# Issuing the retention products of two key tiles and two heads as one run of four, and the group norm's small products further back

## The chip, the cores and the metric

The kernel runs on one core of a Trainium2 chip. The metric is the device time of one execution in microseconds (us): the median of three runs before is 1449.22 us (1446.68 to 1450.26). The profile is of one further execution, whose own time is 1448.63 us and whose span, from the first to the last instruction, is 1446.9 us.

Five engines matter, and each works through its own instructions in program order: TensorE (PE in the profile; PEld is its loading of weights), VectorE (DVE), ScalarE (ACT), GpSimd (POOL), and SyncE (SP), which issues the transfers.

## The reference

A two-layer encoder over 512 tokens of width 1024, in 32-bit floats. Layer 0 mixes tokens with retention and with neighbourhood attention, layer 1 with a state-space (SSD) mixer; each is followed by a feed-forward network (FFN). The two places that matter here, cut down:

```python
# layer 0, retention: per head, every query against every key, weighted by a decay
y = bidir_scan(rq, rk, rv, rv, a_f, a_b)          # = (rq rk^T * decay) rv
mu = mean(y); var = mean((y - mu)**2)             # per head
ret_out = silu(rg) * (y - mu) * rsqrt(var + EPS) * ret_gn_g

# layer 1, SSD: after the scan, per group of 512 channels
y = (y + xh * d_skip) * silu(z)
yg = y * rsqrt(mean(y * y over the group) + EPS) * norm_g
out = yg @ w_out
```

## The kernel before

Activations lie with features on partitions and tokens along the row (128 x 512 tiles). A large product (`mm3`, lines 86 to 88) is three products of split operands, so most of PE's time is in those three lines. Weights come in units of 512 KB (`wunit`): a transfer, a split into a high part on ACT (line 81) and a low part on DVE (line 82).

The kernel is written in a language whose scheduler decides the order of instructions on each engine when the program is built: it takes code order as priority, `high_priority` raises it, and an engine takes what it expects to be ready first. On the chip that order is then fixed, and an engine waits at an instruction whose operands aren't there.

**Layer 0** (`mixer0`) goes through four pairs of heads. The table `PAIRS` gives the order of steps of each pair: five projections (`rq rk nk nq rg`), `d` (the decay tables `toep`, lines 410 to 414), `s0..s3` (scores of one key tile, both heads), `v0..v3` (values of that key tile), `a`, `w` and `o` (the neighbourhood attention), and `n` (the norm over a head's 64 rows). A score step (`ret_scores`) makes two 128 x 512 products a head (lines 423, 424) and masks them on DVE into an `sd` tile (line 426); the `sd` tiles share five buffers with the tiles of the attention and the norm. A value step (`ret_values`, line 434) makes one product for each of the two heads, 64 output rows each: head 0 writes partitions 0 to 63 of the accumulator `y`, head 1 writes 64 to 127. The four value steps of a pair add up in `y`. In the trace each such product has two records on PE, with two weight loads.

**Layer 1** (`mixer1`) goes through four groups of eight heads in the order of `SLOTS`. A step `p` (`pair`, line 757) makes eight small products (line 764) for two heads, again 64 rows for each head, then the gate, the square on ACT (line 770) and the sum of squares `sq` on POOL (line 774). With the last pair of a group, `pair` itself goes on to four one-column products `pss` of the sums (line 782), a DVE step (784) and a POOL power (786) that give the factor `r`. The output projection of a group (`out`, `out_tile`) multiplies by `r` when it leaves PSUM (lines 798, 800, 803). For the last group that projection, `r`, the post norm and the next layer's pre norm follow each other at the end of the mixer.

Of the kernel before, what the change touches and what calls it, by code (L numbers as in the profile page):

```python
# [7 lines left out]
F32 = mybir.dt.float32  # L8
# [3 lines left out]
ALU = mybir.AluOpType  # L12
# [3 lines left out]
P = 128  # L16
S = 512
NT = S // P
D = 1024
KD = D // P  # L20
EPS = 1e-6
# [4 lines left out]
class Env:  # L26
# [57 lines left out]
    def mm3(self, out, lh, ll, rh, rl, first, last):  # L84
        mm = self.nc.tensor.matmul
        mm(out, lh, rh, start=first, stop=False)  # L86
        mm(out, ll, rh, start=False, stop=False)  # L87
        mm(out, lh, rl, start=False, stop=last)  # L88

    def proj_fm(self, out, w, c0=0, c1=S):  # L90

# [161 lines left out]
def log1p_exp_neg(E, alloc, z):  # L253
# [24 lines left out]


PAIRS = (  # L280
# [4 lines left out]
)  # L285


def mixer0(E, w0, w_v, w_fm, tabs, dist_d, logit, gn, bias, w_out, g_post_row, done):
# [3 lines left out]
    nc, tc = E.nc, E.tc  # L292
    with ExitStack() as ctx:
        pool = lambda name, bufs: ctx.enter_context(tc.tile_pool(name=name, bufs=bufs))
        one, two, sd, bp = pool("m0", 1), pool("m0b", 2), pool("m0s", 5), pool("m0n", 2)

        rot = one.tile([P, 2, S], F32, name="rot")
        nc.sync.dma_start(rot, tabs)
# [118 lines left out]
        def ret_scores(p, o, i):  # L417

            o["sd", i] = []
            for h in range(2):  # L420
                ps = E.px.tile([P, S], F32, name="sc", tag="px")
                kt, (qt, ql) = o["rk"][h][:, i * P:(i + 1) * P], o["rq"]
                nc.tensor.matmul(ps, kt, qt[h], start=True, stop=False)
                nc.tensor.matmul(ps, kt, ql[h], start=False, stop=True)
                m = sd.tile([P, S], F32, name="sd", tag="sd")
                nc.vector.tensor_tensor(m, ps, o["toep"][h][:, 384 - i * P:384 - i * P + S], op=ALU.mult)
                o["sd", i].append(m)

        def ret_values(p, o, i):
            if i == 0:  # L430
                o["ry"] = E.px.tile([P, S], F32, name="y", tag="px")
            for h in range(2):
                c = (2 * p + h) * 64
                nc.tensor.matmul(o["ry"][h * 64:h * 64 + 64], rv[:, i, c:c + 64], o["sd", i][h],  # L434
                                 start=i == 0, stop=i == NT - 1)

        def ret_norm(p, o):
            y = o["ry"]
# [82 lines left out]


SLOTS = (
# [4 lines left out]
)  # L528

# [5 lines left out]
def mixer1(E, w_dt, w_fm, cw, dtc, cols, mask, w_out, g_post_row, done):  # L535
# [7 lines left out]
    with ExitStack() as ctx:  # L543
# [168 lines left out]
        def head(o, j):  # L712

            g = o["g"]
            h = g * HPG + j
            pb = [three.tile([P, S], F32, name="pb", bufs=3) for _ in range(2)]
            for dr in range(2):
                nc.sync.dma_start(pb[dr], pd[dr * H + h].partition_broadcast(P))
            e = three.tile([P, NT, C], F32, name="e")
            ds = ys.tile([P, NT, C], F32, name="ds")  # L720
            for c in range(NT):
                cc = slice(c * C, (c + 1) * C)
                nc.scalar.activation(e[:, c], pb[0][:, cc], AF.Identity, scale=-1.0, bias=tok[:, 0, c, h:h + 1])  # L723
                nc.vector.scalar_tensor_tensor(e[:, c], pb[1][:, cc], tok[:, 0, c, H + h:H + h + 1], e[:, c],
                                               op0=ALU.subtract, op1=ALU.max)
                nc.scalar.activation(ds[:, c], um, AF.Identity, scale=ddt[:, c, h:h + 1], bias=tok[:, 1, c, H + h:H + h + 1])  # L726
            nc.scalar.activation(e, e, AF.Exp, scale=-1.0)
            nc.vector.tensor_tensor(e, e, o["gt"], op=ALU.mult)
            nc.vector.tensor_tensor(e, e, ds, op=ALU.mult)  # L729
            o["m"][j] = e  # L730

        def inter(o, q):

# [23 lines left out]
        def pair(o, q):  # L757

            f = o["g"] * 4 + q
            y = o["yi"][q]  # L760
            py = E.px.tile([P, S], F32, name="py", tag="px")
            for c in range(NT):
                for j in range(2):
                    nc.tensor.matmul(py[j * 64:j * 64 + 64, c * C:(c + 1) * C],
                                     o["x"][:, c, (2 * q + j) * 64:(2 * q + j + 1) * 64], o["m"][2 * q + j][:, c],
                                     start=True, stop=True)
            nc.vector.tensor_tensor(y, py, y, op=ALU.add)
            nc.vector.tensor_tensor(y, y, o["t"][6 + q], op=ALU.mult)
            sq = (last if q == 0 else E.tmp).tile([P, S], F32, name="sq", tag="ssq" if q == 0 else "tmp")
# [6 lines left out]
            nc.scalar.activation(yh, y, AF.Identity, scale=col[:, 1, f:f + 1])  # L776
            nc.vector.scalar_tensor_tensor(yl, y, col[:, 1, f:f + 1], yh.bitcast(F32), op0=ALU.mult, op1=ALU.subtract)
            o["y"].append((yh, yl))
            if q == 3:
                pss = E.px.tile([P, NT], F32, name="pss", tag="px")  # L780
                for c in range(NT):
                    nc.tensor.matmul(pss[:, c:c + 1], o["sq"][:, c * C:(c + 1) * C], mean, start=True, stop=True)
                ss = few.tile([P, NT], F32, name="ss", bufs=2)
                nc.vector.tensor_scalar(ss, pss, EPS, None, op0=ALU.add)
                o["r"] = few.tile([P, NT], F32, name="rg", bufs=2)
                nc.gpsimd.tensor_tensor(o["r"], ss, E.mhalf.broadcast_to([P, NT]), op=ALU.pow)

        def out_tile(o, n, t, ws, fin=None):
            g = o["g"]
            ns = slice(n * 512, n * 512 + 512)  # L790
            ps = E.mm.tile([P, 512], F32, name="mm")
            tt = slice(t * P, (t + 1) * P)
            for k in range(4):
                yh, yl = o["y"][k]
                E.mm3(ps, yh[:, tt], yl[:, tt], *ws[k], k == 0, k == 3)
            acc, r = E.x[:, t, ns], o["r"][:, t:t + 1]
            if g == 0:
                nc.scalar.activation(acc, ps, AF.Identity, scale=r)
# [31 lines left out]
        for g, o in enumerate(gs):  # L830
            nx = gs[g + 1] if g + 1 < NG else None
            for step in SLOTS[g].split():
# [8 lines left out]
                elif a == "h":  # L841
                    head(o, i)
                elif a == "i":
                    inter(o, i)
                elif a == "p":
                    pair(o, i)
                elif a == "t":
                    project(o, i)
                elif a == "n":
                    project(nx, i)  # L850
                else:
                    silus(o if a == "S" else nx)
# [3 lines left out]
        def fin(t, n, m):  # L856
# [3 lines left out]
        xt = two.tile([P, 4, 512], R32, name="wo", tag="xt")  # L860
        ws = [E.wunit(w_out[NG - 1, 0, 0]) + E.wunit(w_out[NG - 1, 0, 1]),
              E.wunit(w_out[NG - 1, 1, 0], t4(one, ("state00", "state10", "state01", "state11"))) + E.wunit(w_out[NG - 1, 1, 1], [xt[:, i] for i in range(4)])]
        for t in range(NT):
            for n in range(2):
                out_tile(gs[-1], n, t, ws[n], fin)
            E.finish(TAIL[t], st, done)
        E.late.append(lambda: E.finish(LATE, st, done))

# [143 lines left out]
```

## Time and profile before

| | |
|---|---|
| median of three runs | 1449.22 us |
| the profiled execution | 1448.63 us |
| its span | 1446.9 us |
| layer 0's mixer, from the first scores to its last output product | 88 to 274 us |
| first FFN | 274 to 640 us |
| layer 1's mixer | 665 to 1072 us |
| second FFN, to the end | 1072 to 1447 us |
| records of line 434 / 764 / 782 on PE | 64 / 256 / 32 |

The profile's page gives the busy time of each engine over the span, then groups of instructions by line with the time that the engine stood idle before them and who released it. A timeline row has the start (us from the span's start), the length, the engine, the line, and `xN` for N records merged; records on PE overlap, since an instruction's record goes on after the next has started.

### The profile page before, as it was taken

To read this page: it belongs to the slowest core of one execution; us is meant where nothing else is said; L and a number is where in the kernel's file an instruction comes from. 1 tells how busy PE (TensorE), PEld (TensorE's weight loads), DVE (VectorE), ACT (ScalarE), POOL (GpSimd) and SP (SyncE) were. 2 spreads that over 40 slices of the span, in tenths; PEclk is the share of its full clock that TensorE was granted. 3 is DMA by queue.
4 is the path that set the end of the run, shared out by engine and by line. 5 is a ranking of instruction groups with operands and counts; after the bars stand their busy time and mean duration, and the time that the engine had idled before them with its cause. 6 is when DMAs were issued, how large, how long until landed. Compare 5 with 4: busy or idle time off the path is not lost.

```text
span 1446.9 us, 18038 instructions
## 1 busy us (share of the span) xinstructions
PE 1411.8 (98%) x6848; PEld 1145.2 (79%) x6848; DVE 952.4 (66%) x1484; ACT 724.5 (50%) x1190; POOL 63.0 (4%) x67
## 2 busy tenths in 40 slices
PE   7999999999999999999999999999889999999998
PEld 6877776798888888878688787777778888888886
DVE  7378787766656652347889796899886565564233
ACT  4356665454444441234787775667645444443221
POOL 0010110000000000000000000000020000000000
PEclk9999999999999999999999999999999999999999
DMA  7443221243333323233456354255532333323232
GB/s 253 154 134 88 84 81 44 93 129 91 99 102 90 100 88 109 85 127 114 132 181 180 120 160 145 89 153 156 164 109 84 102 88 102 101 88 102 87 102 88
DMA packets 56951, 166.35 MB, mean 115 GB/s; under 512 B 7200, under 2 KB 7968, under 8 KB 56864
## 3 DMA queue, kind: packets, MB, share of 16 engines
q1 hardware_dynamic: 56864, 165.20, 37.4%
q8 instruction: 54, 0.88, 0.3%
q14 instruction: 33, 0.27, 0.1%
HBM read 157.57 MB, written 5.51 MB: 113 GB/s over the span
## 4 chain that ended last, share of the span: by engine, by line
PE 79%; DVE 9%; ACT 5%; DMA 4%; issue 2%; POOL 1%; SPq 0%; DVEq 0%; POOLq 0%; ACTq 0%
PE mm L86 24%; PE mm L88 24%; PE mm L87 24%; DMA pb<-pd 2%; PE y L434 2%; DVE wlo L82 1%; PE st L701 1%; DVE xf L665 1%; PE pi L745 1%; DMA wst<-in_c_fm 1%; ACT ds L726 1%; PE pt L133 1%; POOL sq L774 1%; ACT whi L81 1%; DVE x L168 1%
## 5 line engine op out<-in xcount | busy, mean ns | idle before, releaser
L86 PE MATMUL mm<-xh,whi 128*128 128x512 f32 (+2 forms) x1216 | 464.3, 382 | 2.3 <-ACT xh L81 1.0
L87 PE MATMUL mm<-xh,wlo 128*128 128x512 f32 (+2 forms) x1216 | 463.6, 381 | 0.7 <-DVE wlo L82 0.7
L88 PE MATMUL mm<-xl,whi 128*128 128x512 f32 (+2 forms) x1216 | 463.5, 382 | 0.0
L82 DVE TENSOR_TENSOR wlo<-wst,whi 128x1024 fp32r<-128x1024 f32 (+1 forms) x214 | 263.5, 1232 | 218.4 <-ACT whi L81 216.0
L81 ACT CAST whi<-wst 128x1024 fp32r<-128x1024 f32 (+1 forms) x214 | 223.6, 1045 | 213.2 <-PE mm L87 156.1
L86 PEld LDWEIGHTS mm<-xh,whi 128*128 128x128 f32 (+1 forms) x1216 | 228.8, 188 | 48.7 <-issue 4.1
L87 PEld LDWEIGHTS mm<-xh,wlo 128*128 128x128 f32 (+1 forms) x1216 | 228.9, 188 | 45.4 <-DVE wlo L82 1.6
L88 PEld LDWEIGHTS mm<-xl,whi 128*128 128x128 f32 (+1 forms) x1216 | 228.2, 188 | 45.9 <-issue 2.9
L218 DVE SCALAR_TENSOR_TENSOR cv<-mm,cwt,cv 128x511 f32<-128x511 f32 x88 | 65.7, 746 | 94.9 <-ACT cv L217 94.9
L86 PE MATMUL mm<-whi,hh 128*128 128x512 f32 x320 | 124.7, 390 | 0.0
L87 PE MATMUL mm<-whi,hl 128*128 128x512 f32 x320 | 124.6, 389 | 0.0
L88 PE MATMUL mm<-wlo,hh 128*128 128x512 f32 x320 | 124.5, 389 | 0.0
L217 ACT ACTIVATE cv<-mm,cwt 128x512 f32<-128x512 f32 x88 | 68.5, 779 | 38.6 <-PE mm L88 38.6
L81 ACT CAST hh<-cv 128x512 fp32r<-128x512 f32 x44 | 27.3, 621 | 100.1 <-DVE cv L226 99.9
L224 ACT ACTIVATE cv<-cv 128x512 f32<-128x512 f32 x44 | 27.8, 632 | 85.8 <-DVE cv L219 85.8
L86 PEld LDWEIGHTS mm<-whi,hh 128*128 128x128 f32 x320 | 60.1, 188 | 12.5
L87 PEld LDWEIGHTS mm<-whi,hl 128*128 128x128 f32 x320 | 60.1, 188 | 12.4
L88 PEld LDWEIGHTS mm<-wlo,hh 128*128 128x128 f32 x320 | 60.1, 188 | 12.3
L219 DVE SCALAR_TENSOR_TENSOR cv<-mm,cwt,cv 128x511 f32<-128x511 f32 x88 | 65.9, 749 | 3.0
L726 ACT ACTIVATE ds<-um,tok,ddt 128x128 f32<-128x128 f32 x128 | 55.7, 484 | 16.6 <-DVE e L729 16.2
L723 ACT ACTIVATE e<-pb,tok 128x128 f32<-128x128 f32 x128 | 42.8, 393 | 15.6 <-DMA pb<-pd 15.1
L82 DVE TENSOR_TENSOR hl<-cv,hh 128x512 fp32r<-128x512 f32 x44 | 30.5, 693 | 28.9 <-ACT hh L81 28.9
(236 smaller groups left out, 1902.3 us busy)
## 6 DMA issues: line engine op xcount, KB each, us to landing
wst<-in_f_up SPq DMA_DIRECT2D x88, 512.0 KB
wst<-in_f_down SPq DMA_DIRECT2D x44, 512.0 KB
wst<-in_c_fm SPq DMA_DIRECT2D x40, 512.0 KB
pb<-pd SPq DMA_DIRECT2D x64, 256.0 KB
wst<-in_ab_fm SPq DMA_DIRECT2D x20, 512.0 KB
gain<-yd SPq DMA_DIRECT2D x32, 256.0 KB
wst<-in_c_out SPq DMA_DIRECT2D x16, 512.0 KB
gain<-in_norms SPq DMA_DIRECT2D x8, 512.0 KB
```

What stands on the lines that cost most here:

```text
L81: self.nc.scalar.copy(hi, src)
L82: self.nc.vector.tensor_tensor(lo, src, hi.bitcast(F32), op=ALU.subtract)
L86: mm(out, lh, rh, start=first, stop=False)
L87: mm(out, ll, rh, start=False, stop=False)
L88: mm(out, lh, rl, start=False, stop=last)
L217: nc.scalar.activation(o, ps, AF.Identity, scale=w(1), bias=w(3))
L218: nc.vector.scalar_tensor_tensor(o[:, 1:], ps[:, :S - 1], w(0), o[:, 1:], op0=ALU.mult, op1=ALU.add)
L219: nc.vector.scalar_tensor_tensor(o[:, :S - 1], ps[:, 1:], w(2), o[:, :S - 1], op0=ALU.mult, op1=ALU.add)
L224: nc.scalar.activation(g, g, AF.Gelu_apprx_tanh)
L434: nc.tensor.matmul(o["ry"][h * 64:h * 64 + 64], rv[:, i, c:c + 64], o["sd", i][h], start=i == 0, stop=i == NT - 1)
L723: nc.scalar.activation(e[:, c], pb[0][:, cc], AF.Identity, scale=-1.0, bias=tok[:, 0, c, h:h + 1])
L726: nc.scalar.activation(ds[:, c], um, AF.Identity, scale=ddt[:, c, h:h + 1], bias=tok[:, 1, c, H + h:H + h + 1])
```

## The change

The value steps `v0` to `v3` become `v0` and `v2`: each makes the four products of two key tiles and two heads, raised in priority by 150. A new helper `together` makes each of the four depend on all four masks (the DVE instructions of line 426), so that none is ready before the others. The steps `v1` and `v3` leave the table, and `v0` now stands behind `a1`. The pool of `sd` tiles has seven buffers in place of five. In layer 1 each of a pair's eight products waits for the decay tiles of both heads. The four `pss` products with what follows leave `pair` and become a step `r` of their own, near the end of each group; in the last group they stand behind the products of the first two output tiles.

```diff
+    def together(self, products, inputs):
+        for m in products:
+            for i in inputs:
+                self.tc.add_manual_dep(m.ins, i.ins.name, mybir.DependencyInfo(
+                    mybir.DependencyClass.Sync, mybir.DependencyReason.DATA))
...
-    "nq rq rk nk rg d s1 s0 a0 v0 a1 v1 w0 s3 s2 a2 v2 a3 w1 w2 v3 n w3 o",
+    "nq rq rk nk rg d s1 s0 a0 a1 v0 w0 s3 s2 a2 a3 v2 w1 w2 n w3 o",
...
-        one, two, sd, bp = pool("m0", 1), pool("m0b", 2), pool("m0s", 5), pool("m0n", 2)
+        one, two, sd, bp = pool("m0", 1), pool("m0b", 2), pool("m0s", 7), pool("m0n", 2)
...
         def ret_values(p, o, i):
+
             if i == 0:
                 o["ry"] = E.px.tile([P, S], F32, name="y", tag="px")
-            for h in range(2):
-                c = (2 * p + h) * 64
-                nc.tensor.matmul(o["ry"][h * 64:h * 64 + 64], rv[:, i, c:c + 64], o["sd", i][h],
-                                 start=i == 0, stop=i == NT - 1)
+            ms, ws = [], []
+            with tc.high_priority(150):
+                for j in (i, i + 1):
+                    for h in range(2):
+                        c = (2 * p + h) * 64
+                        m, w = o["sd", j][h]
+                        ms.append(nc.tensor.matmul(o["ry"][h * 64:h * 64 + 64], rv[:, j, c:c + 64], m,
+                                                   start=j == 0, stop=j == NT - 1))
+                        ws.append(w)
+            E.together(ms, ws)
...
-    "G s0 s1 t6 t7 s2 i0 h0 t8 t9 S h1 p0 i1 n0 h2 h4 h3 p1 i2 n6 n1 h5 n7 i3 n9 p2 N n3 n4 n2 n5 h6 h7 p3 n8 N",
+    "G s0 s1 t6 t7 s2 i0 h0 t8 t9 S h1 p0 i1 n0 h2 h4 h3 p1 i2 n6 n1 h5 n7 i3 n9 p2 N n3 n4 n2 n5 h6 h7 p3 n8 r N",
...
+            ms = [o["m"][2 * q + j] for j in range(2)]
             for c in range(NT):
                 for j in range(2):
-                    nc.tensor.matmul(py[j * 64:j * 64 + 64, c * C:(c + 1) * C],
+                    E.together([nc.tensor.matmul(py[j * 64:j * 64 + 64, c * C:(c + 1) * C],
...
-            if q == 3:
-                pss = E.px.tile([P, NT], F32, name="pss", tag="px")
...
+        def rms(o):
...
+        first = [out_mm(gs[-1], 0, ws[n]) for n in range(2)]
+        rms(gs[-1])
         for t in range(NT):
             for n in range(2):
-                out_tile(gs[-1], n, t, ws[n], fin)
+                out_tile(gs[-1], n, t, ws[n], fin, first[n] if t == 0 else None)
```

On PE, in the second pair of heads (pairs are counted from 0 in what follows, so this is pair 1) at its key tiles 2 and 3, the program before has these rows (`sc` are scores of the neighbourhood attention, `mm` a projection, `pt` transposes, `y<-sd,rv` the value products):

```order
L434 MATMUL y<-sd,rv 64x512
L484 MATMUL pt<-head,e 128x128 x4
L434 MATMUL y<-sd,rv 64x512
L467 MATMUL sc<-nk_1086,nq_1124 128x256
L468 MATMUL sc<-nkl_566,nq_1124 128x256
L467 MATMUL sc<-nk_1086,nq_1124 128x256
L468 MATMUL sc<-nkl_566,nq_1124 128x256
L434 MATMUL y<-sd,rv 64x512
```

And the changed program, at the same place:

```order
L87 MATMUL mm<-xh,wlo 128x512
L88 MATMUL mm<-xl,whi 128x512
L446 MATMUL y<-sd,rv 64x512 x4
L481 MATMUL sc<-nk_1086,nq_1124 128x256
L482 MATMUL sc<-nkl_566,nq_1124 128x256
L481 MATMUL sc<-nk_1086,nq_1124 128x256
L482 MATMUL sc<-nkl_566,nq_1124 128x256
L498 MATMUL pt<-head,e 128x128 x4
```

A fourth lone product stands nine rows above the first piece; the four are one row of four now. In the whole program the 32 value products stood in 22 stretches (5, 6, 6 and 5 in the four pairs; thirteen of them hold a single product, eight hold two, one holds three) and now stand in 8 stretches of four.

On DVE, in pair 2 at its key tiles 2 and 3, the masks `sd` stand before among the maxima (`e,mx`) of the attention:

```order
L486 COPY w<-pt 128x512
L426 TENSOR_TENSOR sd<-sc,toep 128x512 x2
L469 ISA e,mx<-sc,nbias 128x256
L469 ISA mx 128x1
L426 TENSOR_TENSOR sd<-sc,toep 128x512
L469 ISA e,mx<-sc,nbias 128x256
L469 ISA mx 128x1
L426 TENSOR_TENSOR sd<-sc,toep 128x512
```

And in the changed program:

```order
L500 COPY w<-pt 128x512
L490 TENSOR_SCALAR e<-e,sm 128x256 x2
L433 TENSOR_TENSOR sd<-sc,toep 128x512 x2
L483 ISA e,mx<-sc,nbias 128x256
L483 ISA mx 128x1
L433 TENSOR_TENSOR sd<-sc,toep 128x512
L483 ISA e,mx<-sc,nbias 128x256
L483 ISA mx 128x1
L433 TENSOR_TENSOR sd<-sc,toep 128x512
```

The masks keep their places among the maxima; ahead of them a scaling of `e` has moved behind the copy `w`. Around it the DVE order is nearly the same as before.

On PE, at the end of the last group of layer 1 (`yh`, `yl` the gated values, `wo` and `whi` weights of the output projection), the program before has:

```order
L86 MATMUL mm<-wo,yh 128x512
L87 MATMUL mm<-whi,yl 128x512
L88 MATMUL mm<-wlo,yh 128x512
L782 MATMUL pss<-mean,sq 128x1 x4
L86 MATMUL mm<-whi,yh 128x512
```

And the changed program:

```order
L87 MATMUL mm<-whi,yl 128x512
L88 MATMUL mm<-wlo,yh 128x512
L87 MATMUL mm<-wo,yl 128x512
L86 MATMUL mm<-whi,yh 128x512
L88 MATMUL mm<-wo,yh 128x512
L86 MATMUL mm<-wo,yh 128x512
L87 MATMUL mm<-whi,yl 128x512
L88 MATMUL mm<-wlo,yh 128x512
L87 MATMUL mm<-wo,yl 128x512
L88 MATMUL mm<-wo,yh 128x512
L798 MATMUL pss<-mean,sq 128x1 x4
```

The four `pss` products stand 38 large products behind the group's last pair where they stood 30 behind it. In groups 0, 1 and 2 the large products between the last pair and `pss` are 24, 24 and 18 where they were 18, 20 and 19. Of the 16 pairs of layer 1, three were cut into one and seven products before; one still is.

More of the change, by code (lines that the diff above doesn't have):

```diff
@@ L425, in ret_scores @@
                 m = sd.tile([P, S], F32, name="sd", tag="sd")
-                nc.vector.tensor_tensor(m, ps, o["toep"][h][:, 384 - i * P:384 - i * P + S], op=ALU.mult)
-                o["sd", i].append(m)
+                w = nc.vector.tensor_tensor(m, ps, o["toep"][h][:, 384 - i * P:384 - i * P + S], op=ALU.mult)
+                o["sd", i].append((m, w))
         def ret_values(p, o, i):
@@ L728, in head @@
             nc.vector.tensor_tensor(e, e, o["gt"], op=ALU.mult)
-            nc.vector.tensor_tensor(e, e, ds, op=ALU.mult)
-            o["m"][j] = e
+            o["m"][j] = e, nc.vector.tensor_tensor(e, e, ds, op=ALU.mult)
         def inter(o, q):
@@ L761, in pair @@
             py = E.px.tile([P, S], F32, name="py", tag="px")
+            ms = [o["m"][2 * q + j] for j in range(2)]
             for c in range(NT):
                 for j in range(2):
-                    nc.tensor.matmul(py[j * 64:j * 64 + 64, c * C:(c + 1) * C],
-                                     o["x"][:, c, (2 * q + j) * 64:(2 * q + j + 1) * 64], o["m"][2 * q + j][:, c],
-                                     start=True, stop=True)
+                    E.together([nc.tensor.matmul(py[j * 64:j * 64 + 64, c * C:(c + 1) * C],
+                                                 o["x"][:, c, (2 * q + j) * 64:(2 * q + j + 1) * 64], ms[j][0][:, c],
+                                                 start=True, stop=True)], [w for _, w in ms])
             nc.vector.tensor_tensor(y, py, y, op=ALU.add)
@@ L778, in pair, with out_mm @@
             o["y"].append((yh, yl))
-            if q == 3:
-                pss = E.px.tile([P, NT], F32, name="pss", tag="px")
[L781 to L790, printed above, removed]
+        def rms(o):
+            pss = E.px.tile([P, NT], F32, name="pss", tag="px")
+            for c in range(NT):
+                nc.tensor.matmul(pss[:, c:c + 1], o["sq"][:, c * C:(c + 1) * C], mean, start=True, stop=True)
+            ss = few.tile([P, NT], F32, name="ss", bufs=2)
+            nc.vector.tensor_scalar(ss, pss, EPS, None, op0=ALU.add)
+            o["r"] = few.tile([P, NT], F32, name="rg", bufs=2)
+            nc.gpsimd.tensor_tensor(o["r"], ss, E.mhalf.broadcast_to([P, NT]), op=ALU.pow)
+        def out_mm(o, t, ws):
             ps = E.mm.tile([P, 512], F32, name="mm")
@@ L795, in out_tile @@
                 E.mm3(ps, yh[:, tt], yl[:, tt], *ws[k], k == 0, k == 3)
+            return ps
+        def out_tile(o, n, t, ws, fin=None, ps=None):
+            g = o["g"]
+            ns = slice(n * 512, n * 512 + 512)
+            if ps is None:
+                ps = out_mm(o, t, ws)
             acc, r = E.x[:, t, ns], o["r"][:, t:t + 1]
@@ L846, in mixer1 @@
                     pair(o, i)
+                elif a == "r":
+                    rms(o)
                 elif a == "t":
```

10 rows, old and new, of tables (PAIRS, SLOTS) are left out of this document.

## The prediction

> **What bounds the kernel now.** I read the page's busy times and the waits of PE, then the mixer of layer 0 cut at the first masks of each pair of heads.
>
> ```profile
> PE 1411.8 (98%) x6848; PEld 1145.2 (79%) x6848; DVE 952.4 (66%) x1484; ACT 724.5 (50%) x1190; POOL 63.0 (4%) x67
> PE 79%; DVE 9%; ACT 5%; DMA 4%; issue 2%; POOL 1%; SPq 0%; DVEq 0%; POOLq 0%; ACTq 0%
> ```
>
> The first row is the page's busy time by engine, the second the share of each in the chain that ended last. PE bounds the kernel, so time taken from PE counts as far as another engine keeps up. The stretches 88:133, 133:179 and 179:225 are about the first three pairs:
>
> ```profile
> 88.00:133.00 45.00, 45.00 (x222) 32.54 (x222) 37.01 (x70) 29.94 (x51) 4.62 (x3) 1.00 0.35 104
> 133.00:179.00 46.00, 45.72 (x221) 32.59 (x220) 36.61 (x67) 26.41 (x46) 4.75 (x3) 1.00 0.29 80
> 179.00:225.00 46.00, 45.91 (x219) 32.25 (x217) 38.58 (x69) 29.99 (x53) 4.10 (x3) 1.00 0.31 92
> ```
>
> After the length come the busy times of PE, PEld, DVE, ACT and POOL, then PE's clock and the share and rate of the transfers. PE is never idle to speak of, the clock is full and transfers use a third of their engines. DVE is the second engine, with 7 to 9 us idle in each.
>
> **What a stretch of value products costs.** The PE timeline shows a lone product, a couple and a triple:
>
> ```profile
> 143.04 0.39 PE L86 MATMUL mm<-xh,whi 128*128 128x512 f32 x1
> 143.36 1.07 PE L434 MATMUL y<-sd,rv 128*64 128x512 f32 x2
> 144.36 0.38 PE L467 MATMUL sc<-nk,nq 128*128 128x256 f32 x1
> 144.59 0.28 PE L468 MATMUL sc<-nkl,nq 128*128 128x256 f32 x1
> ...
> 228.29 0.39 PE L86 MATMUL mm<-whi,xh 128*128 128x512 f32 x1
> 228.61 1.08 PE L434 MATMUL y<-sd,rv 128*64 128x512 f32 x4
> 229.62 0.38 PE L467 MATMUL sc<-nk,nq 128*128 128x256 f32 x1
> 229.84 0.28 PE L468 MATMUL sc<-nkl,nq 128*128 128x256 f32 x1
> 230.04 1.93 PE L434 MATMUL y<-sd,rv 128*64 128x512 f32 x6
> 231.91 0.38 PE L467 MATMUL sc<-nk,nq 128*128 128x256 f32 x1
> 232.13 0.28 PE L468 MATMUL sc<-nkl,nq 128*128 128x256 f32 x1
> 232.25 0.29 PE L467 MATMUL sc<-nk,nq 128*128 128x256 f32 x1
> ```
>
> A product has two records. Starts tell what a thing occupies: undisturbed, a 128 x 256 product takes 0.12 us (232.13 to 232.25), and a 128 x 512 one by the same rate 0.23. From 143.04 to 144.59 are 1.55 us; less 0.23 and 0.12 for the neighbours, the lone product takes **1.20 us**, the gaps of about 0.1 on both sides included. From 228.29 to 229.84 it is the same 1.20 us for two products: the second head runs beside the first. From 229.84 to 232.13 it is 2.29 less twice 0.12, **2.05 us** for three. So a second round adds 0.85 us, and a fourth product should lie beside the third: I take 2.05 us for a run of four. Eight runs are 16.4 us.
>
> What stands there now, by pair, on line 434 alone:
>
> ```profile
> 88.00:133.00 45.00, 5.48 (x16) 1.07 (x16) 1.00 0.35 104
> 133.00:179.00 46.00, 6.77 (x16) 1.34 (x16) 1.00 0.29 80
> 179.00:228.00 49.00, 6.99 (x16) 1.34 (x16) 1.00 0.29 87
> 228.00:255.00 27.00, 6.23 (x16) 1.24 (x16) 1.00 0.07 20
> ```
>
> The busy sum (second figure) leaves out 0.13 us a stretch (1.20 against 1.07). With 5, 6, 6 and 5 stretches the pairs cost 6.1, 7.6, 7.8 and 6.9 us, 28.4 in all; each becomes 4.1. **Taken from PE: 2.0, 3.5, 3.7 and 2.8, together 12.0 us.** This includes short waits within couples for the second head's mask.
>
> **What of this other engines take back.** In pair 2, DVE and then PE at the end of the pair:
>
> ```profile
> 177.47 2.48 DVE L426 TENSOR_TENSOR sd<-sc,toep 128x512 f32<-128x512 f32 x4
> 187.99 1.27 DVE L426 TENSOR_TENSOR sd<-sc,toep 128x512 f32<-128x512 f32 x2
> 190.94 0.69 DVE L426 TENSOR_TENSOR sd<-sc,toep 128x512 f32<-128x512 f32 x1 [1.33 <-PE y L434]
> 192.87 0.69 DVE L426 TENSOR_TENSOR sd<-sc,toep 128x512 f32<-128x512 f32 x1 [0.90 <-PE y L434]
> 197.98 2.22 DVE L413 SCALAR_TENSOR_TENSOR toep<-dist,lg,toep 128x896 f32<-128x896 f32 x1
> 220.81 3.31 DVE L82 TENSOR_TENSOR xl<-cat,xh 128x512 fp32r<-128x512 f32 x5
> 225.61 0.50 PE L423 MATMUL sc<-rq,rk 128*128 128x512 f32 x1 [0.59 <-DVE sd L426]
> ```
>
> The brackets give idle time and its releaser. From 198 to 225.6 DVE works almost without a gap, and PE already waits 0.59 us for it at the scores of pair 3. Those 27 us can't shrink. Only DVE's idle time ahead of 198 can: some of it was for buffers that value products held (1.33 and 0.90), which now go, but the scores that DVE waits for come earlier only as far as PE stands earlier. The loss lies between nothing and the whole 3.7; I take 1.7. Pair 1 has 9.4 us of DVE idle time, so a smaller 0.6 (between 0 and 3.5). Pair 3 ends in a chain from the last masks through norm and attention to the output projection, with little left on PE to fill it: 0.6 (between 0 and 2.8).
>
> **The wait that is added** is for four masks rather than one. At the first two key tiles the four masks follow each other on DVE (the row at 177.47: four in 2.48 us), and PE has more than that ahead of the run, ten scores and five projections: nothing. At tiles 2 and 3 the rows above show the masks spread from 187.99 to 193.56. Behind the run stand further attention scores, and then DVE, which waits for those. The scheduler has put the run behind the scores and two to five other products; between no wait and about 2.5 us each I take 0.25, about half of the 0.59 us that PE waits for a mask in the row at 225.61. Four such are 1.0 us. Layer 0 gives 12.0 - 1.7 - 0.6 - 0.6 - 1.0 = **8.1 us**, and the FFN behind it, where PE works without a gap, passes it on.
>
> [...]
>
> **Layer 1.** The small products and the cut pairs:
>
> ```profile
> 740.65 0.43 PE L764 MATMUL py<-e,xt 128*64 128x128 f32 x2
> ...
> 796.91 1.05 PE L782 MATMUL pss<-mean,sq 128*128 128x1 f32 x8 [1.10 <-POOL sq L774]
> ...
> 891.63 1.05 PE L782 MATMUL pss<-mean,sq 128*128 128x1 f32 x8 [0.43 <-POOL sq L774]
> ...
> 974.19 0.43 PE L764 MATMUL py<-e,xt 128*64 128x128 f32 x2
> ...
> 981.27 1.05 PE L782 MATMUL pss<-mean,sq 128*128 128x1 f32 x8 [0.43 <-POOL sq L774]
> ...
> 1051.83 1.05 PE L782 MATMUL pss<-mean,sq 128*128 128x1 f32 x8 [0.40 <-POOL sq L774]
> ```
>
> In group 0 six more large products (1.4 us) stand ahead of `pss`, more than its wait of 1.10: gone. In group 1 four more (0.9) against 0.43: gone. In group 2 there is one fewer: kept. Two lone products that were cut from their pair rejoin it: 0.43 and the two gaps of 0.1, 0.6 each. Removed: 1.10 + 0.43 + 1.2 = 2.7 us of PE. At the end of group 3 it goes the other way:
>
> ```profile
> 1053.16 1.02 POOL L786 TENSOR_TENSOR rg<-ss,head 128x4 f32<-128x4 f32 x1 [1.39 <-DVE ss L784]
> 1054.87 1.41 DVE L803 SCALAR_TENSOR_TENSOR m<-mm,rg,x 128x512 f32<-128x512 f32 x2 [1.78 <-PE mm L88]
> 1071.76 1.75 PE L133 MATMUL pt<-head,xs 128*128 128x128 f32 x8 [2.11 <-DVE xs L124]
> ```
>
> Eight more products are 1.8 us, of which the wait of 0.40 covers some: `pss` comes 1.4 us later. Before, its result was ready at about 1054.2 (POOL's power, 1053.16 and 1.02), while `m` had to wait for PE until 1054.87; 0.7 us of slack, so `m` comes **0.7 us later**. From there to 1071.76 the chain is DVE's, and PE waits there: its own gain is lost and the 0.7 added. Net 2.0 us. How much arrives is bounded by DVE:
>
> ```profile
> 950.00:1000.00 50.00, 48.96 (x249) 38.07 (x248) 47.29 (x81) 39.61 (x74) 4.95 (x3) 1.00 0.44 129
> 1000.00:1050.00 50.00, 45.34 (x253) 36.36 (x251) 45.72 (x83) 30.75 (x62) 3.48 (x2) 0.97 0.58 174
> ```
>
> In these stretches it is busy 47.3 and 45.7 of 50 us. I take 1.1 of the 2.0, between -0.7 and 2.7.
>
> **The sum**: 8.1 + 1.1 = 9.2 us. The profiled execution would go from 1448.63 to 1439.4; the median lies 0.6 above that execution, so the forecast is 1449.22 - 9.2 = **1440.0 us**.
>
> **The rivals.** *Everything arrives*: no engine takes anything back, 12.0 + 2.7 = 14.7 us, 1434.5. For it speaks that DVE has idle time in each pair; against it that PE waits for DVE at the start of pairs 2 and 3 already. *DVE becomes the bound*: each pair from 1 on keeps DVE's length; only pair 0's 2.0, half of pairs 1 and 3 (3.2) and none of pair 2 or layer 1 arrive, less 1.0 for waits: 4.2 us, 1445.0. For it speaks the solid stretch from 198; against it the 9 us of idle time in pair 1. *Slower*: PE reaches the runs at tiles 2 and 3 when only the first two masks are there. Masks spread over 5.6 us, two of them done after 1.3, leave a wait of up to 4.3 us, in which the projections stand still and DVE's next scores aren't made; four such are 17.2 in place of the 1.0, which gives 1456.2. It decides from 2.6 us each (9.2 + 1.0 over four); for over 0.3% slower it takes 3.6. Against it: the scheduler set all scores of both tiles ahead of each run. *No effect*: were the four not in parallel on the chip though they are in one row, eight runs of four rounds would be 8 x 3.8 = 30 us, 2 more than now, and with layer 1's 1.1 about 1450. The triple speaks against it.
>
> *Weight loads exposed*: if in each run's second round the loads couldn't start under the first round, four loads of 0.134 us
>
> ```profile
> L434 PEld LDWEIGHTS y<-sd,rv 128*64 128x64 f32 x64 | 5.0, 134 | 6.9 <-issue 4.1 <-DVE sd L426 1.4 <-DVE e L476 0.4
> ```
>
> would come on top, 0.54 a run, 4.3 in all: 1444.3. [...]
>
> **How the numbers follow.** Forecast (1436 to 1443) 0.62; everything arrives 0.11; DVE the bound (1443 to 1447) 0.14; loads exposed 0.05; no effect 0.04; slower 0.04. The range from 1435.0 to 1446.0 leaves out most of "everything arrives" below, and above it the upper part of "DVE the bound", no effect and slower: under 2 in 10. About 0.3% (4.3 us, a bound of 1444.9) is what a measurement of this kernel can tell from no change. Faster by more: 0.62 + 0.11 + 0.08 + 0.04 = 0.85. Slower by more: 0.04. The rest, 0.11, is the same.
>
> **What would show it.** Line 446 on PE in eight stretches of about 1.94 us busy, 15.5 in all; shorter means that records are missing, longer that masks or loads are late. The layer 0 mixer shorter by about 8 us at the first transposes of the FFN (274 now), and idle time of PE at the first scores of pair 3 grown to 2 us, released by DVE. No wait of `pss` in groups 0 and 1, and the first `m` of the tail about 0.7 us later behind the last pair. I'd be wrong by most if DVE's stretch ahead of each pair's scores sets the length of the pairs, or if runs at tiles 2 and 3 wait over 1 us.

## The result, and the profile after

The changed kernel takes **1439.09 us** (median of four runs, 1438.11 to 1440.20) against 1449.74 us for the kernel before on the same chip (four runs, 1446.68 to 1451.47): a ratio of **0.9925, interval 0.9906 to 0.9944**, or 10.6 us. Its profiled execution took 1439.84 us, with a span of 1438.1.

The page of the changed kernel, first the busy time by engine, then the shares of the chain that ended last:

```profile
PE 1402.9 (98%) x6848; PEld 1145.9 (80%) x6848; DVE 947.7 (66%) x1484; ACT 723.2 (50%) x1190; POOL 62.1 (4%) x67
PE 80%; DVE 8%; ACT 4%; DMA 4%; issue 2%; POOL 1%; SPq 0%; DVEq 0%; POOLq 0%; ACTq 0%
```

PE still bounds it and is busy 8.9 us less; DVE too, by 4.7 us, though no DVE instruction was taken out. The same four pairs of layer 0, cut at the first scores of each and, last, at the first transposes of the FFN. Before:

```profile
86.91:130.80 43.89, 43.89 (x216) 31.58 (x215) 36.50 (x69) 29.47 (x50) 4.62 (x3) 1.00 0.36 104
130.80:176.06 45.26, 45.26 (x219) 32.49 (x218) 35.27 (x65) 25.04 (x45) 4.75 (x3) 1.00 0.29 85
176.06:222.37 46.31, 45.94 (x219) 32.36 (x218) 38.89 (x69) 30.30 (x52) 4.10 (x3) 1.00 0.32 92
222.37:274.57 52.20, 50.45 (x243) 36.55 (x242) 36.00 (x71) 24.77 (x51) 2.65 (x3) 1.00 0.21 67
```

And after:

```profile
86.70:128.87 42.17, 42.05 (x216) 31.50 (x215) 35.93 (x69) 28.86 (x49) 4.65 (x3) 1.00 0.32 94
128.87:172.35 43.48, 42.78 (x219) 32.09 (x218) 35.23 (x67) 25.34 (x45) 5.08 (x3) 1.00 0.35 102
172.35:215.66 43.31, 43.02 (x219) 32.21 (x218) 35.67 (x68) 30.34 (x51) 4.64 (x3) 1.00 0.36 98
215.66:265.71 50.05, 47.99 (x244) 36.10 (x242) 35.80 (x71) 24.31 (x51) 2.64 (x3) 1.00 0.23 71
```

The pairs became 1.72, 1.78, 3.00 and 2.15 us shorter, 8.65 together. In pair 1 PE now stands idle for 0.7 us, where it stood never. In pair 2 the fourth figure is the one to see: DVE is busy 3.2 us less, 0.7 of it because one `nq` instruction now falls ahead of the window. The first FFN behind passes all of it on: its first transposes to those of the pre norm of layer 1 are 366.3 us before and 366.5 after.

The value products alone, in the same pairs after the change, and one run of four with its neighbours (eight records):

```profile
87.00:129.00 42.00, 3.88 (x16) 0.97 (x16) 1.00 0.31 94
129.00:172.00 43.00, 3.87 (x16) 0.97 (x16) 1.00 0.35 103
172.00:216.00 44.00, 3.87 (x16) 0.97 (x16) 1.00 0.36 99
216.00:266.00 50.00, 3.87 (x16) 0.97 (x16) 1.00 0.22 68
```

```profile
132.13 0.39 PE L87 MATMUL mm<-xh,wlo 128*128 128x512 f32 x1
132.45 1.94 PE L446 MATMUL y<-sd,rv 128*64 128x512 f32 x8
134.32 0.40 PE L481 MATMUL sc<-nk,nq 128*128 128x256 f32 x1
134.55 0.29 PE L482 MATMUL sc<-nkl,nq 128*128 128x256 f32 x1
```

Every pair is alike: two runs of 1.94 us, 15.5 in all. From 132.13 to 134.55 are 2.42 us; less 0.23 and 0.12 for the neighbours a run takes 2.07, gaps included. The view of that line names no idle time ahead of it: PE waits for masks at none of the eight.

In layer 1 PE's waits for the sums of squares at `pss`, from the view of that tile on PE (us in all, times), before and after:

```profile
  POOL sq L774: 2.4, 4
```

```profile
  POOL sq L788: 1.8, 2
```

Two of four waits went; in this execution the first group's stayed (0.89 us, 1.10 before) and the third's grew from 0.43 to 0.86. The tail of the last group after the change, from the timeline:

```profile
1045.01 1.02 POOL L802 TENSOR_TENSOR rg<-ss,head 128x4 f32<-128x4 f32 x1 [3.02 <-DVE ss L800]
...
1046.06 1.41 DVE L824 SCALAR_TENSOR_TENSOR m<-mm,rg,x 128x512 f32<-128x512 f32 x2 [1.13 <-POOL rg L802]
```

`m` now waits for POOL, not for PE as it did at 1054.87. From the last start of a `py` product it stands 14.5 us behind (13.4 before). The mixer of layer 1, from the pre norm's last transposes to the FFN's first, is 403.1 us before and 403.0 after.

### The profile page after: what moved, and what is told of

It is laid out like the page before. It is cut to its first block, busy times and chain, and to the rows that moved or that the text cites. A ratio compares the mean times of both kernels' runs of the same rounds, so it can differ in the third digit from the quotient of the medians.

```text
span 1438.1 us, 18044 instructions
## 1 busy us (share of the span) xinstructions
PE 1402.9 (98%) x6848; PEld 1145.9 (80%) x6848; DVE 947.7 (66%) x1484; ACT 723.2 (50%) x1190; POOL 62.1 (4%) x67
## 4 chain that ended last, share of the span: by engine, by line
PE 80%; DVE 8%; ACT 4%; DMA 4%; issue 2%; POOL 1%; SPq 0%; DVEq 0%; POOLq 0%; ACTq 0%
PE mm L87 24%; PE mm L86 24%; PE mm L88 24%; DMA pb<-pd 2%; DVE wlo L82 1%; PE st L715 1%; DVE xf L679 1%; PE y L446 1%; PE pi L758 1%; PE pt L140 1%; DMA wst<-in_c_out 1%; DVE x L175 1%; DMA wst<-in_c_fm 1%; PE pt L659 1%; PE py L778 1%
```

## The experiments

Each experiment was compared with the kernel before on its own chip. "Layer 0" is the stretch from the first scores to the FFN's first transposes, as in the windows above; "value products" is what they take of PE, counted from the starts as in the prediction: gaps included, less 0.23 us for a 512-column neighbour, 0.12 for one of 256 and 0.06 for a transpose (half of 0.12, an estimate). The chips differ: the kernel before has medians of 1448.0 to 1449.7 us on them, so a difference of medians from two chips can be off by that much; the ratios are free of it.

| kernel | stretches | value products, us | layer 0, us | median, us | ratio to before |
|---|---|---|---|---|---|
| before | 22 | 28.5 | 187.7 | 1449.5 | 1 |
| e6_buffers_only | 22 | 27.7 | 186.0 | 1447.50 | 0.9989 (0.998 to 0.9999) |
| e11_no_priority | 15 | 24.4 | 183.8 | 1443.06 | 0.9959 (0.9947 to 0.9971) |
| the change | 8 | 16.6 | 179.0 | 1439.09 | 0.9925 (0.9906 to 0.9944) |
| e11_change_again | 8 | 16.6 | 179.4 | 1439.07 | 0.9931 (0.9912 to 0.9951) |
| e1_layer0_only | 8 | 16.6 | 178.6 | 1440.50 | 0.9944 (0.9921 to 0.9966) |
| e4_heads_apart | 8 | 16.7 | 178.8 | 1438.63 | 0.9929 (0.9908 to 0.9951) |
| e2_layer1_only | 22 | 28.5 | 187.5 | 1447.88 | 0.9994 (0.9981 to 1.0007) |

### Either layer alone

`e1_layer0_only` has `mixer1` and `SLOTS` as before, `e2_layer1_only` all of `mixer0` and `PAIRS` as before.

> Only layer 0's part of the change; layer 1 as before. Theory A (layer 0 carries the gain, layer 1's part came to nothing): before less the 8.7 us that the layer 0 mixer became shorter, about 1440.8 us, and the mixer of layer 0 ends where it does in the changed kernel (first FFN transposes at 265.7 us). Theory B (layer 0 gave the 8.1 us and layer 1 the 1.1 us that the prediction had): 1441.4 us and layer 1's mixer again 400.9 us long. Theory C (the clock): after PE's idle time of 3.5 us in the last group of layer 1 the granted clock is 0.5 for 2.8 us before and for 9.6 us in the changed kernel; if that depends on the moment and not on the order, it will be some third length here, and layer 1's mixer will be as much longer or shorter as half of it.

> Only layer 1's part of the change; layer 0 as before. Theory A (what PE gained there other engines took back): 1449.5 us, no difference, and layer 1's mixer 400.8 us long whatever the clock does. Theory B (the prediction): 1448.4. Theory C (PE did gain, and lost it to the clock): layer 1's mixer less its loss to a granted clock under 1 was 400.9 - 3.4 = 397.5 us before and 400.8 - 6.8 = 394.0 in the changed kernel; here it comes out near 394 too, and the whole kernel gains what the clock leaves of 3.5 us, 0 to 3.5 us.

Layer 0 alone carries nearly all: its stretch is 8.9 us shorter than in `e2_layer1_only`, the FFN's first transposes come at 265.8 us as in the change, and the median is 1440.50. Theories A (1440.8) and B (1441.4) lie too near each other to be told apart by it: the ratio's interval is a gain of 4.9 to 11.5 us. Layer 1 alone gives 1.6 us by the medians, 0.9 by the ratio, with an interval that holds no difference. From its first product, as the expectations count, layer 1's mixer took 397.4 us with the new code and 399.8 with the old, where the profiles of the change and of before have 400.8 and 400.9. The clock lost 1.7 us in `e2_layer1_only`, which leaves 395.7, between theory A's and theory C's values; so more was needed (below).

### What joins the run, and what it gains

`e11_no_priority` takes only the raised priority away; the scheduler then splits all but one of the runs:

```diff
-            with tc.high_priority(150):
+            if True:
```

> The changed kernel without the raised priority: the dependency on all four masks stays, but the eight runs come apart into 15 stretches (seven of one product, six... of three, two of two and one of four among them; by pair 4, 4, 4 and 3 stretches). Theory (a stretch of one or two costs 1.2 us of PE, of three or four 2.05): 23.9 us in place of 16.4, 7.5 us of PE, of which 5 to 7 arrive: 1444 to 1446. Rival (it is the dependency and the two more buffers that gained, not the joining): 1439 to 1440.

`e6_buffers_only` is the kernel before with more buffers:

```diff
-        one, two, sd, bp = pool("m0", 1), pool("m0b", 2), pool("m0s", 5), pool("m0n", 2)
+        one, two, sd, bp = pool("m0", 1), pool("m0b", 2), pool("m0s", 7), pool("m0n", 2)
```

> The kernel before with seven sd buffers in place of five, nothing else. Its value products stand in 22 stretches as before. Theory (the joining gains, the buffers only make it possible): 1449.5, and layer 0's mixer ends at 274 to 275 us. Rival (five buffers made DVE wait for value products, 2.2 us in pair 2, and that is what went): 2 to 4 us less, 1446 to 1447.5.

In `e11_no_priority` a split run reads so on PE:

```profile
135.11 0.39 PE L87 MATMUL mm<-xh,wlo 128*128 128x512 f32 x1
135.43 1.07 PE L446 MATMUL y<-sd,rv 128*64 128x512 f32 x2
136.43 0.40 PE L481 MATMUL sc<-nk,nq 128*128 128x256 f32 x1
136.66 0.30 PE L482 MATMUL sc<-nkl,nq 128*128 128x256 f32 x1
...
136.92 0.29 PE L482 MATMUL sc<-nkl,nq 128*128 128x256 f32 x1
137.15 1.93 PE L446 MATMUL y<-sd,rv 128*64 128x512 f32 x6
139.01 0.50 PE L430 MATMUL sc<-rq,rk 128*128 128x512 f32 x1
139.34 0.39 PE L431 MATMUL sc<-rql,rk 128*128 128x512 f32 x1
```

The columns are start, length, engine, line and operation. From 135.11 to 136.66 are 1.55 us, less 0.23 and 0.12 for the neighbours 1.20 for the lone product; from 136.92 to 139.34 are 2.42, less the same 2.07 for the other three: what all four take in one run. The 15 stretches (six of one product, two of two, six of three and one of four) took 24.4 us against 23.9 expected, 7.7 more than the eight; 4.8 of them were in layer 0's length and 4.0 in the median (4.9 by the ratios), a little under the 5 to 7 expected and far from the rival. So the dependency and the buffers don't do it alone. The buffers do gain something of their own, 1.6 us of layer 0 and 1.8 of the time (0.1 to 2.9 by the ratio's interval), at the lower edge of the rival's 2 to 4. From the kernel before to the change layer 0 becomes 0.73 us shorter for each us that value products leave PE, (187.7 - 179.0) / (28.5 - 16.6). Without the part of the buffers, from `e6_buffers_only` on, it is 0.63: (186.0 - 179.0) / (27.7 - 16.6).

### The order inside the run

`e4_heads_apart` issues both key tiles of head 0, then both of head 1:

```diff
-                for j in (i, i + 1):
-                    for h in range(2):
+                for h in range(2):
+                    for j in (i, i + 1):
```

> The changed kernel with the four products of a run in another order: both key tiles of head 0, then both of head 1. Theory (the second head runs beside the first only where the two stand next to each other): three rounds for two, a run takes 2.9 us where it takes 2.1, eight runs cost 6.8 us more of PE and the kernel about 1444 to 1446. Rival (products of different output partitions run beside each other whatever their order): no loss, 1439. Rival (none run beside each other, and the gain had another cause): the same 2.1 us a run, 1439, with the records of both heads one after the other.

```profile
91.26 0.39 PE L86 MATMUL mm<-xh,whi 128*128 128x512 f32 x1
91.58 1.95 PE L446 MATMUL y<-sd,rv 128*64 128x512 f32 x8
93.45 0.39 PE L481 MATMUL sc<-nk,nq 128*128 128x256 f32 x1
93.67 0.28 PE L482 MATMUL sc<-nkl,nq 128*128 128x256 f32 x1
```

The theory fell: the run takes 1.95 us (1.94 in the change) and the kernel the same time (1438.63 us, 1439.09 in the change). So a run of four took the time of two rounds here whichever head's products stood next to each other. Where the four cost more they stood apart, with 128*128 products between them: 1.20 and 2.07 us in the rows of `e11_no_priority`, 3.27 together.

### DVE and POOL

`e5_pool_more` gives POOL more to do beside the rotation, `e9_rotate_on_dve` takes the rotation from it:

```diff
+        spare = one.tile([P, 352], F32, name="spare")
...
                 nc.gpsimd.tensor_tensor(b, b, rot[:, 1], op=ALU.mult)
+                for _ in range(2):
+                    nc.gpsimd.tensor_tensor(spare, b[:, :352], rot[:, 1, :352], op=ALU.mult)
```

```diff
-                nc.gpsimd.tensor_tensor(b, b, rot[:, 1], op=ALU.mult)
+                nc.vector.tensor_tensor(b, b, rot[:, 1], op=ALU.mult)
```

> The changed kernel with sixteen more GpSimd products of 128x352 in layer 0's mixer, two behind each rotation product; nobody reads them. Theory (a DVE instruction that meets a POOL one is held for up to the POOL one's length): by the traces DVE's instructions beside POOL ones were 7.9 us longer than their like elsewhere before the change and 4.0 us after it, which is where pair 2 gained the 1.3 us more than forecast; here sixteen times 0.9 us stand in its way, the lengthening grows from 4.0 to 8 to 13 us, and layer 0's mixer, 265.7 us to its end, becomes 1 to 5 us longer: 1440 to 1444. Rival (POOL is idle for 96% of the time and its work is free): DVE's durations as they were, 1439.

> The changed kernel with the rotation products of layer 0 (128x512, 1.3 us each on POOL, eight in all) on DVE in POOL's place. Theory (a DVE instruction and a POOL one hold each other up): DVE takes on 8 x 0.68 = 5.4 us and loses most of the 4.0 us by which its instructions were longer beside POOL's; its busy time from the first scores to the first FFN transposes goes from 142.6 to 143.5 to 145 us, that stretch (179.0 us) to 179 to 181: 1439 to 1441. Rival (POOL's work cost DVE nothing; e5_pool_more was slower because the sums behind the rotation came later): DVE 148 us, the stretch 183 to 184, 1443 to 1445.

The timeline of `e5_pool_more` in pair 1, all engines, a few rows:

```profile
149.85 2.26 POOL L402 TENSOR_TENSOR rb<-rb,rot 128x512 f32<-128x512 f32 x1 [25.29 <-DMA rb<-ra]
...
150.95 1.71 DVE L405 TENSOR_TENSOR ra<-ra,rot 128x512 f32<-128x512 f32 x1
...
152.19 2.26 POOL L404 TENSOR_TENSOR spare<-rb,rot 128x352 f32<-128x352 f32 x2
...
152.58 2.02 DVE L493 TENSOR_SCALAR e<-e,sm 128x256 f32<-128x256 f32 x2
...
153.74 0.41 PE L501 MATMUL pt<-head,e 128*128 128x128 f32 x2 [1.21 <-DVE e L493]
...
154.66 0.44 PE L501 MATMUL pt<-head,e 128*128 128x128 f32 x2 [0.51 <-DVE e L493]
```

The two scalings take 2.02 us where they take 0.60 alone, the product `ra` 1.71 where it takes 0.69, and PE waits 1.7 us for them at the transposes. The median was 1443.73 us, 4.6 more than the change, and layer 0 182.2 us: the theory's time, though its size was off (DVE's busy time in layer 0 rose by 3.7 us, from 142.6 to 146.3, not by 4 to 9, with no DVE instruction added). So in this run DVE's instructions took longer where they met POOL's.

In `e9_rotate_on_dve` DVE took on eight products of about 0.67 us, 5.4 in all. The median was 1440.38 us, as the theory had it and 3 us under the rival. The theory's other figure came true too: DVE's busy time in layer 0 rose by only 1.7 us, to 144.4. But that isn't the release that the theory meant. Some work stands ahead of the first scores here, which come at 91.3 us. So the window leaves out two of the eight products, which it would in the change as well, and two more DVE instructions (a `wlo` and an `nkl`) that it holds in the change; its layer 0, 177.9 us, isn't comparable. From the start of the program to the FFN's first transposes DVE is busy 194.1 us, against 189.9 in the change and 190.9 in its second profile. So of the 5.4 us that DVE took on, 3 to 4 stayed, and only about 1 to 2 of the 4.0 by which its instructions were longer went; POOL's product `rs` is still there (from 123.28 to 124.82 us, where DVE has no idle time). What this run does show is that 3 to 4 us more on DVE cost the kernel about 1 us (1440.38, and 1439.07 for the change on the same chip).

```diff
-                nc.vector.tensor_scalar(e[:, j], e[:, j], sm[:, j:j + 1], None, op0=ALU.mult)
+                nc.scalar.activation(e[:, j], e[:, j], AF.Identity, scale=sm[:, j:j + 1])
```

> The changed kernel with the scaling of the attention's weights by the inverse sum (32 instructions of 128x256, 0.35 us each on DVE) on ACT. Theory (DVE shares the bound of layer 0 with PE: 3.7 us more on DVE made e5_pool_more's layer 0 3.2 us longer): DVE's busy time in layer 0's mixer goes from 142.6 to about 131 us, the stretch from the first scores to the first FFN transposes from 179.0 to between 173 and 177, the kernel to 1433 to 1437. Rival (PE alone bounds it, and pairs 1 to 3 lost their part to something else): 178 to 179 and 1439. Rival (ACT's queue, 109 us busy there, makes the weights late): 180 or more.

Here, in `e10_scale_on_act`, the theory fell. DVE was busy 135.5 us in layer 0, 7.2 less than in the change, and the stretch took 179.2 us and the kernel 1439.49 (ratio 0.9933, 0.9913 to 0.9953): no gain. ACT took over 14.0 us (122.9 where it had 108.9), and PE waited for it at one of the transposes (0.36 us), so a small gain on DVE may have been lost there. But with `e9_rotate_on_dve` it says that DVE's load alone isn't a bound of layer 0. `e5_pool_more` was slower because of where DVE's instructions took longer: PE's waits for `e` at the transposes grew from 0.8 to 2.8 us.

### The clock in layer 1

`e7_busy_gap` fills PE's wait of 3.5 us in the last group with products that nobody reads; `e8_busy_both` fills the wait ahead of the second FFN as well:

```diff
-                pi = E.px.tile([P, 3, C], F32, name="pi", tag="px")
+                pi = E.px.tile([P, 4, C], F32, name="pi", tag="px")
...
+                if g == NG - 1 and q == 3 and dr == 1:
+                    for _ in range(14):
+                        nc.tensor.matmul(pi[:, 3], o["st"][1, 0][:, q * P:(q + 1) * P], o["t"][1][:, :C],
+                                         start=True, stop=True)
...
```

```diff
+            if t == NT - 1:
+                warm = E.mm.tile([P, S], F32, name="mm")
+                for _ in range(12):
+                    with tc.high_priority(1):
+                        nc.tensor.matmul(warm, gs[-1]["y"][0][0][:, :P], ws[1][0][0], start=True, stop=True)
```

> The changed kernel with fourteen idle products (128x128, of data that is there already, into an unused quarter of an accumulator) in PE's wait of 3.5 us in the last group of layer 1. Theory (that wait lowers the clock, for 2.8 to 9.6 us by the moment, and what PE gained in layer 1 is lost there in some executions): the granted clock stays 1.00 there, layer 1's mixer (from the pre norm's last transposes to the FFN's first: 403.1 us in the changed kernel's profile, 399.2 to 399.7 in three others that have the same layer 1) is 396 to 398.5 us long, the median 1437 to 1438.5 and the executions lie closer together. Rival (DVE sets the pace there, the clock is hidden): clock 1.00, length 399 to 400, median 1439. Rival (the wait isn't what lowers the clock): it falls there all the same.

> As e7_busy_gap, with twelve more idle products (128x512 single pass, 0.23 us each) in PE's wait of 3.0 us ahead of the second FFN's first products. Theory: there the clock was 0.5 for 3.4 us in every profile, 1.7 us lost, and the FFN behind it is bound by PE: another 1.0 to 1.7 us, median 1435.5 to 1437.5, and the lowest clock in layer 1 and the second FFN's start is 1.00. Rival (the products delay the transposes they stand ahead of, by more than they gain): 1438 or more.

Around the last group's wait, the changed kernel and then `e7_busy_gap` (behind the busy times stands the granted clock):

```profile
1020.00:1041.00 21.00, 16.98 (x82) 13.60 (x81) 18.17 (x29) 11.43 (x18) 4.08 (x3) 0.76 0.52 166
```

```profile
1024.00:1045.00 21.00, 17.80 (x114) 14.13 (x113) 17.23 (x28) 10.07 (x16) 3.36 (x2) 1.00 0.47 146
```

With the wait the clock was 0.76 in this stretch, with the idle products in it 1.00; so here it was the wait that lowered it. But the time didn't move: medians 1439.81 us (ratio 0.994, 0.992 to 0.9961) and 1440.15 (0.9937, 0.9922 to 0.9952), layer 1's mixer 403.6 and 400.8 us long. From the second group's first products (where the rows below are divided) to its end are 257.2 and 256.5 us, where the kernels with this layer 1 and no idle products have 255.5 to 257.6. `e8_busy_both` kept 1.00 at the second FFN's start as well, and from that FFN's first transposes to the end took 381.2 us, as in the change. So the clock isn't what took layer 1's gain, and the rival's 1439 us was the nearer; that it is DVE that sets the pace there was not tested. To see what spreads layer 1's lengths, one more profile of the change:

> The changed kernel once more, for a second profile of it. From the first scores to the first FFN transposes 178.6 to 179.6 us. Theory (its first profile met a slow execution of layer 1's first group: 170.8 us to the second group's first pair, where four other profiles with the same layer 1 took 167.1 to 167.9): 167 to 168 here, the wait of the first group's pss under 0.4 us, and layer 1's mixer 399 to 400 us. Rival (that is how this kernel runs): 170.8, a wait of 1.1, 403 us.

The mixer of layer 1 cut at the second group's first products: the change, the change again, and `e2_layer1_only`:

```profile
653.78:800.67 146.89, 142.67 (x736) 113.59 (x735) 122.25 (x227) 109.96 (x209) 4.92 (x4) 0.99 0.51 147
800.67:1056.83 256.16, 249.41 (x1290) 200.32 (x1288) 223.19 (x379) 169.09 (x327) 19.88 (x15) 0.98 0.47 139
```

```profile
654.81:799.23 144.42, 140.69 (x736) 112.38 (x735) 122.11 (x226) 110.06 (x209) 4.95 (x4) 1.00 0.51 150
799.23:1056.87 257.64, 249.83 (x1290) 200.15 (x1288) 223.27 (x379) 169.47 (x327) 19.80 (x15) 0.98 0.45 138
```

```profile
662.56:806.23 143.67, 140.83 (x737) 112.53 (x736) 122.32 (x226) 110.03 (x209) 4.93 (x4) 1.00 0.51 151
806.23:1062.23 256.00, 248.01 (x1290) 198.07 (x1288) 222.84 (x379) 169.06 (x327) 19.62 (x15) 0.99 0.45 139
```

The theory was right on the first group (shorter by 2.5 us here, and `pss` didn't wait) and wrong on the whole (402.1 us, not 399 to 400): the rest took 1.5 us longer. The same execution-to-execution spread is there with the old layer 1: its first group took 146.9, 143.8 and 143.8 us in the three profiles that have it (before, `e1_layer0_only`, `e6_buffers_only`), and 143.2 to 146.9 in the ten with the new one. In the rest the three have 256.2 to 258.3 us. One profile of each can't show a gain of 1 us in layer 1.

## Why the prediction was right, step by step

The forecast was 1440.0 us, 9.2 less than before; the change came out at 1439.1, and the range held it. That it is so near is partly luck: the gain by the medians, 10.6 us, has an interval of 8.1 to 13.6, the two profiled executions differ by 8.8, and two errors in the sum for layer 0 cancelled each other (below).

**The cost of a run** was right: 2.05 us forecast, 2.07 measured, busy sum 15.5 in both. The triple's price did carry over to the four. This also settles "no effect" and "weight loads exposed". The loads cost nothing visible in a run of four, which would be 2.6 us with the rival's 0.54: in the run shown with the result (132.45 to 134.39 us) the later ones start at 132.93 and 133.36, while its products go on.

**What is taken from PE** was right: 12.0 us forecast; from the starts 28.5 - 16.6 = 11.9, by pair 2.1, 3.5, 3.7 and 2.7.

**The added wait** was mis-sized: 1.0 us forecast, none measured. The scores that the scheduler set ahead of each second run covered the masks, so the slower rival didn't come near its point of decision.

**What other engines take back** was right in sum only. With the wait the charges were 3.9 us; 11.9 - 8.65 = 3.3 were lost, but as 0.3, 1.7, 0.7 and 0.6 by pair, where the forecast, with a quarter us of wait in each, had 0.25, 0.85, 1.95 and 0.85. Pair 1 lost twice what was charged, and pair 2 lost 1.3 us less; that the sum came out is luck. PE's idle time in the four windows, length less busy time in the rows above, rose from 2.1 to 3.2 us. So 1.1 of the 3.3 are waits that the profile shows; the profile doesn't show where the rest is, and that stays open. Two steps failed.

In pair 2 it was "those 27 us can't shrink". They shrank, because some of DVE's instructions from 198 to 225.6 were longer than the same ones elsewhere. Rows of before, then the same DVE instructions after the change:

```profile
197.96 1.29 POOL L394 TENSOR_TENSOR rb<-rb,rot 128x512 f32<-128x512 f32 x1 [29.44 <-DMA rb<-ra]
...
208.37 2.33 DVE L378 SCALAR_TENSOR_TENSOR rql<-ra,rq 64x512 fp32r<-64x512 f32 x2
...
208.62 1.52 POOL L447 TENSOR_TENSOR rs<-rs,rg 128x512 f32<-128x512 f32 x1 [9.37 <-DVE rs L446]
```

```profile
189.88 1.64 DVE L490 TENSOR_SCALAR e<-e,sm 128x256 f32<-128x256 f32 x2
...
193.66 1.14 DVE L420 SCALAR_TENSOR_TENSOR toep<-dist,lg,toep 128x896 f32<-128x896 f32 x1
...
195.91 1.38 DVE L385 SCALAR_TENSOR_TENSOR rql<-ra,rq 64x512 fp32r<-64x512 f32 x2
```

`rql` took 2.33 us beside POOL's product and 1.38 without it; the `toep` quoted in the prediction at 197.98 stood beside POOL's rotation product and took 2.22, now 1.14. The forecast read a duration beside POOL's product as one of DVE's own work. The lengthening isn't gone: of pair 2's instructions `toep`, `rql` and a product `ra` were 3.1 us longer together before; after the change the two scalings of `e` shown, which take 0.61 elsewhere, and the same `ra` are 1.4 longer. PE's wait at the scores of pair 3 didn't grow to 2 us either; it fell from 0.59 to 0.45.

Which instruction meets POOL is a matter of the schedule, not of the joining. `e6_buffers_only`, with its value products in 22 stretches, has most of pair 2's gain:

```profile
176.11:220.26 44.15, 44.15 (x219) 32.35 (x218) 36.73 (x68) 28.10 (x50) 4.61 (x3) 1.00 0.33 97
```

That is 2.2 of the 3.0 us, with DVE busy 2.2 us less; its pair 3 is 1.7 us longer. So the split by pairs isn't a price of the joining in each; the sum over the four is the safer figure.

In pair 1 the step "9.4 us of DVE idle time, so a smaller 0.6" failed. Idle time on average didn't help: an instruction that took longer beside POOL's (`ra`, 1.70 us) stood in front of one that PE needed. After the change, all engines:

```profile
147.17 2.25 POOL L401 TENSOR_TENSOR rb<-rb,rot 128x512 f32<-128x512 f32 x1 [24.74 <-DMA rb<-ra]
...
148.26 1.70 DVE L402 TENSOR_TENSOR ra<-ra,rot 128x512 f32<-128x512 f32 x1
...
149.90 0.60 DVE L490 TENSOR_SCALAR e<-e,sm 128x256 f32<-128x256 f32 x2
...
150.38 0.30 PE L498 MATMUL pt<-head,e 128*128 128x128 f32 x1 [0.51 <-DVE e L490]
```

`e9_rotate_on_dve` has no POOL product there, and PE doesn't wait at these transposes; but its pair 1 is only 0.25 us shorter (43.23 us), so this wait explains a part of the 1.7 us. All of PE's idle time in pair 1 is 0.7 us, so 1.0 us isn't in waits that the profile shows; where it went stays open.

**"DVE becomes the bound"** is refuted by the change itself: pair 2, of which that rival let nothing arrive, became 3.0 us shorter. `e10_scale_on_act` agrees: 7.2 us less on DVE, no gain.

**Layer 1** can't be settled to the 1.1 us that was counted. The medians put it at 1.4 us (`e1_layer0_only` less the change, from two chips) and 1.6 (`e2_layer1_only`), the latter's ratio at 0.9 with an interval of about -1 to 2.8; the profiles of before and of the change differ there by 0.1; single profiles spread by 3 us in the first group alone. Of its steps, "gone" held for `pss` in group 1 in every profile and in group 0 in most (it waited 0.89 us in that of the change and 1.03 in `e7_busy_gap`), and "kept" in group 2 was 0.4 too low. The tail's 0.7 is not refuted: `m` stood 14.5 to 15.7 us behind the last pair where it had been 13.4 to 14.2, and 1.2 later in the pair of profiles of before and the change.

## What to carry to other kernels

The value products here (128*64, half as wide as the 128*128 ones beside them) cost by the stretch that they stood in: a lone one cost as much as two beside each other (1.20 us), and a run of four 2.07, so 0.87 for the second two; in the other order of `e4_heads_apart` the run was as short (1.95 us busy for 1.94). How much of that arrives, 0.6 to 0.7 of it here, was told badly by how idle DVE is on average (pair 1 had 9.4 us of it and lost 1.7 of its 3.5); a part depends on what stands in its queue ahead of the few results that PE is about to need. Before a stretch of an engine is called incompressible, each instruction's duration there should be set beside the same instruction elsewhere: here one (`rql`, two records) took 2.33 us beside POOL's product and 1.38 without it.

## What the hardware showed besides

**DVE's and POOL's instructions lengthened each other**, a part of them: `ra` 0.69 us alone and 1.70 beside POOL, POOL's own product 1.29 us alone and 2.25 when DVE was first. The one mask (`sd`) that met POOL, with one operand in PSUM, kept its 0.68 us (101.10 us, beside POOL's product at 101.26, which kept its 1.29). The scalings of `e`, which read a single tile, were longer as well (0.35 us alone, 1.38 for the longer of the two at 189.88, beside POOL's product at 190.07). Why some were and the mask wasn't, no run shows.

**Order of products**: in `e4_heads_apart` head 1's first product is third in the program, behind both of head 0. Had these two taken a round each ahead of it, the run would take three rounds, 0.85 us more by the prediction's step from one round to two; it took the 1.95 us of two. That head 1's first went ahead of head 0's second would explain it, but that is the author's reading: the records don't say which product they belong to.

**The clock** fell to 0.5 at the last group's wait of 3.5 us in every profile but the two with idle products there, for 3 to 10 us, and in the profiles of before and of the change also in the first group, behind a wait of 1.10 and 0.89 us (`pss` started at 796.91 and 789.56 us, the clock fell from 799.1 and 791.9 on). That wait alone doesn't decide it: `e6_buffers_only` has it too (1.1 us) and kept 1.00 there. Keeping it at 1.00 in the last group gained nothing that could be measured (1439.81 us, 1439.09 for the change on another chip).
